# A hybrid decoder step: the gate matrix of the dense expert tiles built by accumulating indirect DMAs of single elements into a cleared DRAM tensor instead of by one-hot products

## The chip, the cores and the metric

The kernel runs on one core of one Trainium2 chip. The core has five engines with an instruction queue each: TensorE (PE, matrix products), VectorE (DVE), ScalarE (ACT), GpSimd (POOL) and SyncE (SP, which here only issues DMAs). Each engine works through its own queue in order, and engines wait for each other by semaphores. DMAs move data between DRAM and the on-chip memory; plain ones are issued from SP, those whose addresses come from a table of indices ("indirect") from POOL. The metric is the time of one execution in microseconds (us).

## What is computed

One layer of a decoder trunk for 1024 prompt tokens (8 tiles of 128) and 32 sample tokens (a ninth tile): a mixing block (windowed attention and a gated recurrence), cross-attention, and a feed-forward layer of 16384 one-neuron experts, from which each token takes 16 for each of 8 heads. The change is in this last layer, `peer_ffn`:

```
q  = (x @ w_pq)                                   # per token: 8 heads
s1, s2 = q_left @ k1, q_right @ k2                # 128 + 128 scores per head
v1, i1 = top_k(s1, 16); v2, i2 = top_k(s2, 16)
sc, ci = top_k(v1[:, None] + v2[None, :], 16)     # 16 of the 256 sums
e = i1[ci // 16] * 128 + i2[ci % 16]              # expert numbers, 0 .. 16383
g = softmax(sc)
y = sum over heads and k of  g * gelu(x . peer_u[e]) * peer_v[e]
```

## The kernel before

The tokens go through the first two blocks in three parts, `PARTS = ((0, 1, 2), (3, 4, 8), (5, 6, 7))`. A part has `middle` (attention and recurrence, four rounds) and `tail` (output product, cross-attention, expert scores, and at its end `select_tile` for each tile, which yields the chosen expert numbers and weights). The generators of the parts are interleaved by `run`, and a list scheduler then puts the instructions of the whole program into an order for each engine; on the chip each engine keeps that order.

The expert layer is done in two ways. Tiles 5, 6, 7 and 8 are gathered: `gather_tile` fetches for every one of a token's choices a row of `peer_u` and then of `peer_v` (128 rows of 4 KB in one indirect DMA, issued by POOL, L1177), and DVE takes the dot product (L1184) or adds the scaled row (L1195). That is 32 + 32 such DMAs for tile 8 and 128 + 128 for each of 7, 6 and 5: 832. Tiles 0 to 4 (`DENSE`, 640 tokens) are done densely: `dense` runs over 128 groups of 128 experts; for each it forms `a = u . x` for all 640 tokens (L202 to L204), gelu (ACT, L1082), multiplies by a gate (DVE, L1084: the softmax weight where the token has chosen the expert, otherwise zero) and multiplies with `v` (L1092 to L1094). While PE does this, POOL and DVE do the gathered tiles.

So `dense` needs a gate matrix of 128 x 128 experts by 640 tokens in DRAM (`gtall`, 42 MB). It is built by `gates(di)`, which takes for each dense tile the two key numbers and the weight of every choice (stored by `select_tile` as `selD`, after three PE transposes), and for each token multiplies two one-hot matrices: DVE builds the first for four tokens at once (L1013) and the second, scaled by the weight, for each token (L1018; for some of the tokens of tiles 2 to 4 ACT does that with two instructions, L1021 and L1022), PE multiplies them (L1024), ACT copies the result out of PSUM (L1027), and SP stores it in pieces of 16 tokens (L1030). `run` interleaves tiles 0 to 2 with part 2's `middle` and tiles 3 and 4 with part 2's `tail`. In `dense` the gates come back in pieces of eight groups of experts (`gate_piece`, L1058).

POOL's other work is 25 small `pow` instructions in `rstd_of` (L211), one in each normalization, which later work on DVE and PE waits for.

## Time and profile before

| | before |
|---|---|
| time, median of 3 runs | 3695.17 us (3675.76 to 3701.54) |
| span of the profiled execution | 3704.7 us |
| PE busy | 3390.1 us (92%) |
| DVE busy | 2623.8 us (71%) |
| ACT busy | 1401.8 us (38%) |
| POOL busy | 1102.0 us (30%) |
| bytes moved by DMA | 1007.87 MB |

The profile cuts the span into 40 slices of 92.6 us and gives for each the busy tenths of each engine, the share of full clock granted to PE, and the busy share of the DMA engines. "Stretches" below are the same sums for windows of one's own choice. The timeline lists instructions in order of time, with the idle time of the engine ahead of each and what ended it. The chain is the sequence of work that ended last, followed back from the end.

### The profile page before, as it was taken

What the parts mean: (1) busy time and instruction counts of PE and PEld (TensorE: products, weight loads), DVE (VectorE), ACT (ScalarE), POOL (GpSimd) and SP (SyncE); (2) the same over time, 40 slices, a digit from 0 to 9 for tenths busy, and PEclk for the clock granted to TensorE, in tenths of its full rate; (3) what the DMA queues carried; (4) which work ended last, traced back from release to release, by engine and by line L of the source; (5) the groups of instructions that cost most, each with busy time, mean ns of one, the idle gap of its engine ahead of it and who ended that gap; (6) DMA issues with size and microseconds to landing.
All of it is one profiled execution on the core that took longest, in us unless ns stands there. A gap on an engine that the chain in (4) does not pass through costs nothing.

```text
span 3704.7 us, 53428 instructions
## 1 busy us (share of the span) xinstructions
PE 3390.1 (92%) x19338; PEld 2927.2 (79%) x19338; DVE 2623.8 (71%) x6014; ACT 1401.8 (38%) x2673; POOL 1102.0 (30%) x871
## 2 busy tenths in 40 slices
PE   5999999999999889886889999999999999999991
PEld 4876776677886779776779988998889998899980
DVE  4443333244885777789878868987788987888996
ACT  4544434343444555886332222222222222222220
POOL 0000000000000000011246535654555555555664
PEclk9999999999999889998999999999999999999995
DMA  7667776665656475489679969998898998999997
GB/s 239 227 226 248 235 256 225 204 208 193 204 190 209 151 266 210 175 317 322 226 259 346 346 229 330 346 334 307 309 325 317 347 344 297 330 339 324 340 329 254
DMA packets 408519, 1007.87 MB, mean 272 GB/s; under 512 B 43968, under 2 KB 168896, under 8 KB 406848
## 3 DMA queue, kind: packets, MB, share of 16 engines
q1 hardware_dynamic: 288448, 568.20, 45.1%
q0 software_dynamic: 119808, 436.26, 32.7%
q8 instruction: 152, 2.49, 0.3%
q14 instruction: 111, 0.91, 0.1%
HBM read 866.01 MB, written 138.31 MB: 271 GB/s over the span
## 4 chain that ended last, share of the span: by engine, by line
PE 27%; DMA 10%; issue 7%; DVE 7%; POOL 4%; ACT 1%; SPq 0%; POOLq 0%; DVEq 0%; ACTq 0%
DMA row<-in_peer_v,ix 5%; PE a L204 4%; PE a L202 4%; PE a L203 4%; POOL row L1177 4%; PE y L1094 3%; PE y L1093 2%; PE y L1092 2%; DMA row<-in_peer_u,ix 2%; PE yr L1092 2%; PE yr L1093 2%; PE yr L1094 2%; DMA u<-in_uT 2%; DVE row L1184 2%; DVE ha L1195 1%
## 5 line engine op out<-in xcount | busy, mean ns | idle before, releaser
L1177 POOL DMA_INDIRECT row<-in_peer_u,ix x416 | 526.2, 1265 | 669.2 <-DVE dots L1184 412.5
L1177 POOL DMA_INDIRECT row<-in_peer_v,ix x416 | 546.4, 1314 | 451.4 <-DVE ha L1195 298.7
L202 PE MATMUL a<-xh,u 128*128 128x320 f32 x2048 | 635.8, 310 | 38.2 <-ACT u L170 28.3
L204 PE MATMUL a<-xh,u 128*128 128x320 f32 x2048 | 635.8, 310 | 2.9 <-DVE u L171 2.9
L203 PE MATMUL a<-xl,u 128*128 128x320 f32 x2048 | 635.5, 310 | 0.0
L1195 DVE SCALAR_TENSOR_TENSOR ha<-row,dots,ha 128x1024 f32<-128x1024 f32 x416 | 533.4, 1282 | 77.0 <-DMA row<-in_peer_v,ix 66.4
L1184 DVE CUSTOM_DVE_ANT_0 row<-row,ha 128x1024 f32<-128x1024 f32 x416 | 501.5, 1222 | 119.7 <-DMA row<-in_peer_u,ix 99.6
L211 POOL TENSOR_TENSOR rs_r<-rs_m,mhalf 128x3 f32<-128x3 f32 (+2 forms) x25 | 21.2, 854 | 1381.7 <-DVE rs_m L209 1083.0
L202 PEld LDWEIGHTS a<-xh,u 128*128 128x128 f32 x2048 | 387.6, 189 | 52.0 <-ACT u L170 28.6
L203 PEld LDWEIGHTS a<-xl,u 128*128 128x128 f32 x2048 | 387.3, 189 | 10.2
L204 PEld LDWEIGHTS a<-xh,u 128*128 128x128 f32 x2048 | 387.3, 189 | 3.6 <-DVE u L171 3.3
L202 PE MATMUL z<-zhi,wz 128*128 128x384 f32 (+2 forms) x928 | 329.1, 355 | 25.8 <-ACT zhi L170 10.2
L203 PE MATMUL z<-zlo,wz 128*128 128x384 f32 (+2 forms) x928 | 316.4, 341 | 2.8 <-DVE zlo L171 2.1
L204 PE MATMUL z<-zhi,wz 128*128 128x384 f32 (+2 forms) x928 | 313.2, 338 | 0.0
L1092 PE MATMUL y<-v,w 128*128 128x512 f32 x768 | 300.9, 393 | 12.4 <-ACT w L170 12.4
L170 ACT CAST w<-w 128x320 fp32r<-128x320 f32 x256 | 117.8, 460 | 503.9 <-DVE w L1084 476.9
L1093 PE MATMUL y<-v,w 128*128 128x512 f32 x768 | 301.3, 394 | 0.0
L170 ACT CAST u<-u 128x1024 fp32r<-128x1024 f32 x128 | 134.8, 1053 | 364.0 <-PE a L203 276.7
L1094 PE MATMUL y<-v,w 128*128 128x512 f32 x768 | 253.7, 392 | 6.5 <-DVE w L171 6.5
L1082 ACT ACTIVATE w<-a 128x320 f32<-128x320 f32 x256 | 110.8, 433 | 361.5 <-PE a L204 337.9
L202 PEld LDWEIGHTS z<-zhi,wz 128*128 128x128 f32 x928 | 180.3, 194 | 65.9 <-issue 19.6
L1092 PE MATMUL yr<-v,w 128*128 128x512 f32 x512 | 204.1, 399 | 19.9 <-DVE ys L1121 15.6
(466 smaller groups left out, 6966.0 us busy)
## 6 DMA issues: line engine op xcount, KB each, us to landing
u<-in_uT SPq DMA_DIRECT2D x128, 512.0 KB
v<-in_peer_v SPq DMA_DIRECT2D x128, 512.0 KB
wz<-wd_w_in SPq DMA_DIRECT2D x112, 512.0 KB
gt<-gtall SPq DMA_DIRECT2D x124, 320.0 KB
wd_w_in<-wz SPq DMA_DIRECT2D x56, 512.0 KB
gtall<-sg SPq DMA_DIRECT2D x34, 512.0 KB
wd_w_pq<-wt SPq DMA_DIRECT2D x32, 512.0 KB
wt<-wd_w_pq SPq DMA_DIRECT2D x32, 512.0 KB
```

The lines of the kernel that those rows point to most:

```text
L170: S.copy(hi, src)
L202: PE.matmul(out, lhsT=whi, rhs=xhi[:, c, sl], start=c == 0, stop=False)
L203: PE.matmul(out, lhsT=whi, rhs=xlo[:, c, sl], start=False, stop=False)
L204: ins = PE.matmul(out, lhsT=wlo, rhs=xhi[:, c, sl], start=False, stop=c == kc - 1)
L211: G.tensor_tensor(r, m, mhalf[:, :n], op=ALU.pow)
L1082: S.activation(ga[:, lo:hi], pa, AF.Gelu)
L1092: PE.matmul(o, lhsT=wh[:, sl], rhs=vh[:, ds], start=start and q == 0, stop=False)
L1093: PE.matmul(o, lhsT=wh[:, sl], rhs=vl[:, ds], start=False, stop=False)
L1094: PE.matmul(o, lhsT=wl[:, sl], rhs=vh[:, ds], start=False, stop=stop and q == len(ws) - 1)
L1177: G.indirect_dma_start(out=row, out_offset=None, in_=tab, in_offset=bass.IndirectOffsetOnAxis(ap=col(ix, j), axis=0))
L1184: V.tensor_tensor_reduce(row, row, hn, 1.0, 0.0, op0=ALU.mult, op1=ALU.add, accum_out=col(dots, j))
L1195: V.scalar_tensor_tensor(acc, row, col(dots, j), acc, op0=ALU.mult, op1=ALU.add)
```

## The change

The gate matrix is now one flat DRAM tensor `gates` of 128 * 128 * 640 elements, ordered by second key, first key, token. Three things make it:

- `clear_gates`, behind `memory_kv` in the first part, stores zeros: 80 DMAs of 512 KB from SP.
- `select_tile` computes for the dense tiles a flat element number, (key2 * 128 + key1) * 640 + token, and stores it and the weight (`ixd`, `gd`, which before were for the gathered tiles only). The transposes, the copies of `selD` and `selD` itself are gone.
- `scatter` loads both and issues 128 indirect DMAs for each dense tile, from POOL, each of which adds one element per token (128 elements) to `gates`. The instructions of a tile that belong to different heads can name the same element and must follow each other; those of one head, and of different tiles, are declared not to conflict. The tables `ix` and `gw` have three buffers, which the gathered tiles also use.

In `dense` the gates of a group of experts are now one DMA of 128 rows of 640 elements, and each waits for the last scatters of all five tiles (`added`). `gates`, `LATE`, `iota`, `selD` and `gtall` are gone. `run` now interleaves the clearing with part 0's middle, `scatter` of tiles 0 to 2 behind part 0's tail with part 1's middle, that of tiles 3 and 4 behind part 1's tail with part 2's middle. The rest of the arithmetic is as before.

```diff
+        eu = T(pk, [128, 128], U32, "sc")[:R, :n]
         if t in DENSE:
-            p = bank(SELB)
-            for i in range(3):
-                PE.transpose(out=p[:, i * 128 : (i + 1) * 128], in_=fnd[:, i], identity=ident)
-            st = T(pk, [128, 4, 128], F32, "c2", 2)
-            ...
-            SP.dma_start(selD[DENSE.index(t)], st)
-            return
-        eu = T(pk, [128, 128], U32, "sc")[:R, :n]
-        V.scalar_tensor_tensor(eu, fnd[:, 0], 128.0, fnd[:, 1], op0=ALU.mult, op1=ALU.add)
+            V.scalar_tensor_tensor(fnd[:, 0], fnd[:, 1], 128.0, fnd[:, 0], op0=ALU.mult, op1=ALU.add)
+            V.tensor_scalar(eu, fnd[:, 0], float(NM), col(TOK, DENSE.index(t)), op0=ALU.mult, op1=ALU.add)
+        else:
+            V.scalar_tensor_tensor(eu, fnd[:, 0], 128.0, fnd[:, 1], op0=ALU.mult, op1=ALU.add)
         SP.dma_start(ixd[t][:R, :n], eu)
         SP.dma_start(gd[t][:R, :n], fnd[:, 2])

-    def gates(di):
-        ...
+    def clear_gates():
+        z = T(pk, [128, 8, 128], F32, "tw", 2)
+        V.memset(z, 0.0)
+        rows = gates.rearrange("(n p x) o -> n p (x o)", p=128, x=1024)
+        for n in range(128 * NM // 1024):
+            SP.dma_start(rows[n], z.rearrange("p a b -> p (a b)"))
+            if n % 10 == 9:
                 yield
+
+    def scatter(dis):
+        ins_ = {}
+        for di in dis:
+            ix = T(gat, [128, 128], U32, "ix", 3)
+            gw = T(gat, [128, 128], F32, "gw", 3)
+            SP.dma_start(ix, ixd[DENSE[di]])
+            SP.dma_start(gw, gd[DENSE[di]])
+            ins_[di] = (ix, gw, [])
+        for h in range(8):
+            for di in dis:
+                ix, gw, last = ins_[di]
+                made = []
+                for j in range(16 * h, 16 * h + 16):
+                    ins = G.indirect_dma_start(out=gates, out_offset=bass.IndirectOffsetOnAxis(ap=col(ix, j), axis=0),
+                                               in_=col(gw, j), in_offset=None, compute_op=ALU.add)
+                    for d in range(len(DENSE)):
+                        for k in range(8):
+                            if d != di or k == h:
+                                tc.declare_no_dep(ins.ins, group=f"gates{d}_{k}", reason="no two of these write one element")
+                    for w_ in last:
+                        sync(ins, w_)
+                    made.append(ins)
+                for ins in made:
+                    tc.add_to_no_dep_group(f"gates{di}_{h}", ins.ins)
+                last[:] = made
+            yield
+        for di in dis:
+            added.extend(ins_[di][2])

         def hidden(i, out):
-            ...
+            gt = T(dn, [128, M], F32, "gt", GTB)
+            ins = SP.dma_start(gt, gview[i])
+            for w_ in added:
+                sync(ins, w_)
...
-                V.tensor_tensor(gv, gv, gts[kg, h][:, :, ki], op=ALU.mult)
+                V.tensor_tensor(ga[:, lo:hi], ga[:, lo:hi], gt[:, lo:hi], op=ALU.mult)

-    run(W0, p[0].middle(lambda: ahead(p[1])), memory_kv())
+    run(W0, p[0].middle(lambda: ahead(p[1])), seq_of(memory_kv, clear_gates))
     p[1].first_h()
-    run(W1, p[1].middle(lambda: ahead(p[2])), seq_of(lambda: p[0].tail("T")), seq_of(sample_mix))
+    run(W1, p[1].middle(lambda: ahead(p[2])), seq_of(lambda: p[0].tail("T"), lambda: scatter(range(NG))), seq_of(sample_mix))
     p[2].first_h()
-    run(W2, p[2].middle(), seq_of(lambda: p[1].tail("T")), seq_of(*[lambda i=i: gates(i) for i in range(NG)]))
-    run(W3, p[2].tail("Z"), seq_of(*[lambda i=i: gates(i) for i in range(NG, len(DENSE))]))
+    run(W2, p[2].middle(), seq_of(lambda: p[1].tail("T"), lambda: scatter(range(NG, len(DENSE)))))
+    run((1,), p[2].tail("Z"))
```

How the order on the engines moves is shown at three places.

**POOL, where the gate of tile 0 starts.** Before, POOL has nothing but `pow` instructions (`rs_r`) here, and then the row gathers of tile 8 (`row<-in_peer_u`):

```order
L211 TENSOR_TENSOR rs_r_8159<-rs_m_8157,mhalf_100 128x3
L211 TENSOR_TENSOR rs_r_9296<-rs_m_9294,mhalf_100 128x3
L211 TENSOR_TENSOR rs_r_9424<-rs_m_9422,mhalf_100 128x3
L211 TENSOR_TENSOR rs_r_10016<-rs_m_10014,mhalf_100 128x3
L211 TENSOR_TENSOR rs_r_11019<-rs_m_11017,mhalf_100 128x3
L211 TENSOR_TENSOR rs_r_11866<-rs_m_11864,mhalf_100 128x3
L211 TENSOR_TENSOR rs_r_13384<-rs_m_13382,mhalf_100 128x3
L211 TENSOR_TENSOR rs_r_13991<-rs_m_13989,mhalf_100 128x3
L1177 DMA row_30090<-in_peer_u,ix_30080 128x1024
```

Now, behind the same `pow` instructions (`rs_r_8621` and `rs_r_9516` stand where 8159 and 9296 stood), the scatters begin (`ix_7742` is tile 0's table, `ix_7746` tile 1's). The semaphores in brackets are those that the row waits for; DMASW0 to DMASW7 are raised in turn when DMAs of POOL have landed, so that the row that waits for DMASW1 waits for the scatter of the row ahead of it:

```order
L203 TENSOR_TENSOR rs_r_9516<-rs_m_9514,mhalf_98 128x3 [waits DVE_49,PE_49]
L1001 DMA gates_158<-gw_7743,ix_7742 10485760x1 [waits DMAHW4_49,DMAHW5_49,DMAHW3_49,DMAHW6_49,DMAHW2_49,DMAHW7_49,DMAHW1_49,DMAHW0_49]
L1001 DMA gates_158<-gw_7743,ix_7742 10485760x1 [waits DMASW0_49]
L1001 DMA gates_158<-gw_7743,ix_7742 10485760x1 [waits DMASW1_49]
L1001 DMA gates_158<-gw_7743,ix_7742 10485760x1 [waits DMASW2_49]
L1001 DMA gates_158<-gw_7743,ix_7742 10485760x1 [waits DMASW3_49]
L1001 DMA gates_158<-gw_7743,ix_7742 10485760x1 [waits DMASW4_49]
```

Every scatter of a tile waits until the scatter ahead of it of the same tile has landed (also within a head); scatters of different tiles alternate. Seven more `pow` instructions stand between the scatters, behind 23, 32, 77, 134, 134, 236 and 305 of them; the last is the last one of part 2's tail. Of these 305 scatters 113 are tile 0's, 102 tile 1's and 90 tile 2's. Tile 3's first scatter stands behind tile 0's last, and tile 4's behind tile 1's.

**POOL and DVE, where `dense` starts.** Now the gathers of tile 8 (64) and of tile 7 (133, `ix_28563`) stand between the scatters of tiles 3 and 4 (`ix_12328`, `ix_12332`):

```order
L1001 DMA gates_158<-gw_12329,ix_12328 10485760x1
L1001 DMA gates_158<-gw_12333,ix_12332 10485760x1
L1142 DMA row_28669<-in_peer_u,ix_28563 128x1024
L1142 DMA row_28672<-in_peer_u,ix_28563 128x1024
L1142 DMA row_28582<-in_peer_u,ix_28563 128x1024
L1142 DMA row_28585<-in_peer_u,ix_28563 128x1024
L1001 DMA gates_158<-gw_12329,ix_12328 10485760x1
L1001 DMA gates_158<-gw_12333,ix_12332 10485760x1
```

From the first scatter to the last there are 844 rows on POOL: 640 scatters, 197 gathers and 7 `pow`. Behind the last scatter comes the gate load, and so the first multiplication by a gate, on DVE. Before, it stood here (`w<-w,gt`; `ha<-row` is a gathered row of tile 8's second half, the 37 ahead of it are all that DVE had taken):

```order
L171 TENSOR_TENSOR v_16183<-v_16180,v_16182 128x1024
L1195 SCALAR_TENSOR_TENSOR ha_30186<-row_30203,dots_30089,ha_30186 128x1024
L1084 TENSOR_TENSOR w_16186<-w_16186,gt_16167 128x320
L1195 SCALAR_TENSOR_TENSOR ha_30186<-row_30206,dots_30089,ha_30186 128x1024
L171 TENSOR_TENSOR w_16188<-w_16186,w_16187 128x320
```

Now it stands here, behind 195 gathered rows (all of tile 8's, and all 128 dot products and three additions of tile 7):

```order
L1157 TENSOR_TENSOR dots_28569<-dots_28569,gw_28564 128x128
L1160 SCALAR_TENSOR_TENSOR ha_28954<-row_28958,dots_28569,ha_28954 128x1024
L1160 SCALAR_TENSOR_TENSOR ha_28954<-row_28961,dots_28569,ha_28954 128x1024
L1160 SCALAR_TENSOR_TENSOR ha_28954<-row_28964,dots_28569,ha_28954 128x1024
L1049 TENSOR_TENSOR w_14360<-w_14360,gt_14346 128x320 x2
L1160 SCALAR_TENSOR_TENSOR ha_28954<-row_28967,dots_28569,ha_28954 128x1024
```

**SP, where `gates` is cleared.** Before, the queue has weight loads of part 0 here (`raw`), stores of their split halves (`wd_w_in`), and `t<-yd`, the first load of part 0's tail:

```order
L190 DMA raw_1480<-in_w_in 128x512
L194 DMA wd_w_in_0_368_1477<-wz_1472 128x1024
L190 DMA raw_1515<-in_w_in 128x512
L493 DMA yd_72_170<-gs_503 128x384
L194 DMA wd_w_in_1_371_1484<-wz_1479 128x1024
```

Now the 80 stores of zeros stand between the loads of `w_mv` and that same `t<-yd`, the last 32 of them without a break:

```order
L978 DMA gates_158<-tw_1422 128x1024 x14
L186 DMA wd_w_in_0_355_1440<-wz_1435 128x1024
L182 DMA raw_1478<-in_w_in 128x512
L978 DMA gates_158<-tw_1422 128x1024 x9
L186 DMA wd_w_in_1_358_1447<-wz_1442 128x1024
L182 DMA raw_1485<-in_w_in 128x512
L978 DMA gates_158<-tw_1422 128x1024 x32
L533 DMA t_3399<-yd_66_163 128x384
```

## Rows read from the trace of the kernel before

**Rows 1.** The page: span; POOL's busy tenths and the DMA rate in 40 slices.
```profile
span 3704.7 us, 53428 instructions
...
POOL 0000000000000000011246535654555555555664
...
GB/s 239 227 226 248 235 256 225 204 208 193 204 190 209 151 266 210 175 317 322 226 259 346 346 229 330 346 334 307 309 325 317 347 344 297 330 339 324 340 329 254
```
**Rows 2.** Stretches of the span: busy us of each engine, PE's granted clock, DMA.
```profile
core 0: us, PE busy (x) PEld busy (x) DVE busy (x) ACT busy (x) POOL busy (x), PEclk, DMA share, GB/s
...
1053.00:1300.00 247.00, 222.60 (x1451) 183.54 (x1450) 174.58 (x593) 127.54 (x238) 4.37 (x5) 0.96 0.53 186
1300.00:1470.00 170.00, 153.45 (x1011) 142.69 (x1010) 120.68 (x530) 94.52 (x240) 0.00 (x0) 0.93 0.72 247
1470.00:1600.00 130.00, 109.34 (x690) 100.51 (x688) 99.48 (x303) 109.66 (x261) 11.45 (x10) 0.95 0.58 212
...
1735.00:2100.00 365.00, 320.09 (x1752) 288.98 (x1752) 311.48 (x688) 106.02 (x154) 164.81 (x122) 0.93 0.84 293
...
3300.00:3600.00 300.00, 299.39 (x1680) 272.53 (x1679) 265.13 (x339) 79.19 (x130) 183.16 (x139) 1.00 0.93 333
```
**Rows 3.** Stretches, the one-hot products alone (L1024): their sum over 1053 to 1735 us.
```profile
sum 682.00, PE 193.09 PEld 173.08; mean PE 48.27 PEld 43.27
```
**Rows 4.** Groups by line: busy us, mean ns, idle before and its releasers.
```profile
L1018 DVE TENSOR_SCALAR oh<-iota,x_vs 128x128 f32<-128x128 f32 x448 | 128.7, 343 | 2.8 <-DMA x_vs<-selD 2.8
...
L1013 DVE TENSOR_TENSOR raw<-iota,x_vs 128x512 f32<-128x512 f32 x160 | 110.2, 688 | 84.8 <-PE g L1024 73.9 <-DMA x_vs<-selD 3.7 <-PE x L1024 3.6
...
L1177 POOL DMA_INDIRECT row<-in_peer_v,ix x416 | 546.4, 1314 | 451.4 <-DVE ha L1195 298.7 <-issue 39.7 <-DMA row<-in_peer_v,ix 35.1
```
**Rows 5.** Timeline of SP: start us, us; the stores of tiles 0 and 3.
```profile
1053.27 0.32 SPq L980 DMA_DIRECT2D selD<-c  x1
...
1524.48 0.32 SPq L980 DMA_DIRECT2D selD<-c  x1
```
**Rows 6.** Timeline of POOL: the last normalization of part 2's tail; gathers back to back.
```profile
1570.81 0.90 POOL L211 TENSOR_TENSOR rs_r<-rs_m,mhalf 128x3 f32<-128x3 f32 x1
...
1904.05 0.94 POOL L1177 DMA_INDIRECT row<-in_peer_u,ix  x1 [0.30 <-issue]
1905.30 0.94 POOL L1177 DMA_INDIRECT row<-in_peer_u,ix  x1 [0.30 <-issue]
```
**Rows 7.** The same with little else running: every gather from here is one row.
```profile
3642.87 1.58 POOL L1177 DMA_INDIRECT row<-in_peer_v,ix  x1 [0.19 <-issue]
...
3670.85 1.68 POOL L1177 DMA_INDIRECT row<-in_peer_v,ix  x1 [0.30 <-issue]
```
**Rows 8.** Chain in order of time: start us, us from issue to landing.
```profile
1806.22 6.68 DMA row<-in_peer_v,ix
...
1838.67 3.46 DMA ixd<-sc
...
2220.53 3.98 DMA row<-in_peer_u,ix
```
**Rows 9.** Instructions on `gt` and `yr`: ns min/median/max, first and last start us.
```profile
L1084 DVE TENSOR_TENSOR w<-w,gt x256: 471/485/544, 1776.0 to 3605.2; 128x320 f32<-128x320 f32 x128
...
L1121 DVE TENSOR_TENSOR ys<-ys,yr x130: 665/681/689, 1795.7 to 3624.8; 128x512 f32<-128x512 f32 x130
```
**Rows 10.** Timeline of SP in part 0: two weight loads, and the tail's first load.
```profile
210.67 0.42 SPq L190 DMA_DIRECT2D raw<-in_w_in  x1
222.91 0.32 SPq L194 DMA_DIRECT2D wd_w_in<-wz  x1
...
233.36 0.77 SPq L541 DMA_DIRECT2D t<-yd  x1
```
**Rows 11.** Stretches of part 0, all engines.
```profile
200.00:340.00 140.00, 126.96 (x664) 96.16 (x663) 61.97 (x189) 60.58 (x135) 2.40 (x3) 0.98 0.69 232
340.00:500.00 160.00, 159.91 (x930) 114.85 (x931) 51.90 (x174) 63.40 (x115) 2.37 (x3) 1.00 0.77 247
```

More of the change, by code (lines that the diff above doesn't have):

```diff
@@ L26 @@
 NG = sum(t in PARTS[0] for t in DENSE)
-GT = 16
+NM = 128 * len(DENSE)
 def col(p, n):
@@ L35 @@
 XA = (16, 1)
-GA = (10, 1)
+GTB = 6
 EARLY = 90
@@ L153, in _body @@
     gd = [T(dr, [128, 128], F32, f"gd{t}") for t in range(9)]
-    selD = [T(dr, [128, 4, 128], F32, f"selD{t}") for t in range(len(DENSE))]
     h3x = [T(dr, [128, 8, 128 * len(DENSE)], F32, f"h3x{i}") for i in range(2)]
-    gtall = T(dr, [len(DENSE) * 128 // GT, 128, 128 * GT], F32, "gtall")
+    gates = T(dr, [128 * 128 * NM, 1], F32, "gates")
     accd = T(dr, [128, D], F32, "accd")
-    gtd = [gtall[b].rearrange("p (i t) -> p i t", t=GT) for b in range(len(DENSE) * 128 // GT)]
     mkd = T(dr, [128, 4, 256], F32, "mkd")
@@ L667, in tail @@
                     if smp:
-                        sc4 = T(wk, [128, 2, 128], F32, "sc4")
+                        sc4 = c2([128, 2, 128])
                 q = tq(jc % 2)
@@ L984, in select_tile @@
         SP.dma_start(ixd[t][:R, :n], eu)
         SP.dma_start(gd[t][:R, :n], fnd[:, 2])
-    flips = {}
-    def flip(name, n):
-        flips[name] = flips.get(name, -1) + 1
-        return flips[name] % n
-    def gates(di):
-        st = T(wk, [128, 4, 128], F32, "x_vs")
-        SP.dma_start(st, selD[di])
-        late_ = di >= NG
-        for blk in range(128 // GT):
-            if late_:
-                k = flip("stg", 3)
-                if k < 2:
-                    stg = [T(wk, [128, 128, GT], F32, ("thi", "tlo")[k])]
-                else:
-                    stg = [T(wk, [128, 64, GT], F32, "sg", 2) for i in range(2)]
-            elif flip("stg", 2) or not BIG:
-                stg = [T(wk, [128, 64, GT], F32, "sg", 2) for i in range(2)]
-            else:
-                stg = [T(gat, [128, 64, GT], F32, "row", 2) for i in range(2)]
-            w = 128 // len(stg)
-            for q in range(GT // 4):
-                p = bank(("g", "Ty", "Ts")[flip("gb", LB)] if late_ else "g")
-                t0 = blk * GT + 4 * q
-                hot = [T(wk, [128, 4, 128], F32, "raw" if RAW else "oh", 2 if RAW else 3), T(wk, [128, 4, 128], F32, "oh", 3)]
-                V.tensor_tensor(hot[0], iota.rearrange("p (o k) -> p o k", o=1).to_broadcast([128, 4, 128]),
-                                st[:, 0, t0 : t0 + 4].rearrange("p (t o) -> p t o", o=1)
-                                .to_broadcast([128, 4, 128]), op=ALU.is_equal)
-                for i in range(4):
-                    if i >= LATE[di]:
-                        V.tensor_scalar(hot[1][:, i], iota, col(st[:, 1], t0 + i), col(st[:, 2], t0 + i),
-                                        op0=ALU.is_equal, op1=ALU.mult)
-                    else:
-                        S.activation(hot[1][:, i], iota, AF.Abs, bias=col(st[:, 1], t0 + i), scale=-1.0)
-                        S.activation(hot[1][:, i], hot[1][:, i], AF.Relu, bias=col(st[:, 2], t0 + i),
-                                     scale=col(st[:, 3], t0 + i))
-                    PE.matmul(p[:, i * 128 : (i + 1) * 128], lhsT=hot[0][:, i], rhs=hot[1][:, i],
-                              start=True, stop=True)
-                for i, sg in enumerate(stg):
-                    ANY.tensor_copy(sg[:, :, 4 * q : 4 * q + 4].rearrange("p i t -> p t i"),
-                                    p.rearrange("p (t i) -> p t i", i=128)[:, :, i * w : (i + 1) * w])
-            for i, sg in enumerate(stg):
-                SP.dma_start(gtd[di * (128 // GT) + blk][:, i * w : (i + 1) * w], sg)
-            if blk % 2:
-                yield
@@ new lines, in clear_gates, with sync @@
+    def clear_gates():
[5 more added lines that the diff above has]
+            if n % 10 == 9:
+                yield
+    added = []
+    def sync(ins, to):
+        tc.add_manual_dep(ins.ins, to.ins.name,
+                          mybir.DependencyInfo(mybir.DependencyClass.Sync, mybir.DependencyReason.DATA), reason="gates")
@@ L1077, in hidden @@
                 lo, hi = h * (M // 2), (h + 1) * (M // 2)
-                kg, ki = divmod(i + 4 * h, 8)
-                ki -= 4 * h if kg == 0 else 0
                 pa = T(dps, [128, 512], F32, "a", 6 - 2 * KEEP + 1 if KEEP > 2 else 2)[:, : M // 2]
```

39 lines of the change are left out of this document (6 added, 33 removed).

## The prediction

> **What bounds the kernel now.** I read the page first, for when POOL works and how fast DMA can go, then stretches of the span, then the groups by line, and for single events the timelines, the chain and the view by tile.
>
> POOL does next to nothing in the first 17 of 40 slices and has room later; the fastest slices move 346 GB/s [rows 1]. From 1053 to 1600 us PE is busy 222.60 + 153.45 + 109.34 = 485 of 547 us, with DVE at 72% [rows 2]: a mixed stage in which no engine is full. The one-hot products take 193 us of PE from 1053 to 1735 us [rows 3]; DVE's two lines for them take 128.7 + 110.2 = 239 us [rows 4]. From then on `dense` runs. Its first multiplication by a gate is at 1776.0, and the last product is added at 3624.8 us [rows 9]; deep in it PE is busy 299 of 300 us [rows 2]. The end, at 3704.7 us, is late gathers of tile 5 and the sample's finish. So two questions decide: when can `dense` begin, and how long does it then run.
>
> **What the change takes away.** All of the one-hot work: 193 us of PE, 239 us of DVE, and ACT's share, all between 1053 and 1735 us. If nothing else ended later, `dense` could begin 100 to 190 us earlier: PE's 193 us is the most, and the stretch from 1735 to 2100 us with 45 us of idle PE [rows 2] shows that the start of `dense` has other limits.
>
> **What it adds, 1: clearing.** 80 stores of 512 KB, 42 MB, at the best 346 GB/s [rows 1] are 121 us of transfer. On SP they stand between the `w_mv` loads and `t<-yd`; before, this piece of the queue took from about 211 to 233 us [rows 10]. The weight loads of part 0 are queued behind them. DMA was busy 0.69 there, and from 340 us PE is busy 159.91 of 160 us [rows 11], so a delay isn't made good. Bounds: 0 (all in the gaps) and 121 us; I take 70, since 23 us of the old queue time and some 30 us of work that needs no new weights lie beside it. So the first scatter, which stands behind tile 0's `select_tile` at 1053.27 us [rows 5], can start at about 1053 + 70, say 1125.
>
> **What it adds, 2: 640 scatters on POOL.** Each issues 128 addresses, as a gather does, but 4 bytes for each instead of 4 KB. The trace has no such DMA. Its price has two parts. *Issue*: a gather holds POOL 0.94 us with 0.30 to the next at best [rows 6], 1.31 + 0.30 in the mean [rows 4]. I take 1.24 to 1.37 (a scatter moves almost nothing, but is issued by the same engine in the same form). *Landing*: the shortest landing of a gather that the chain shows is 3.98 us after its issue, another 6.68; a small store to DRAM took 3.46 [rows 8]. For a scatter I take 3.5, nearest to the small store; bounds 2.5 (two issues, if landing costs less) and 6.7.
>
> The order says what these cost. Every scatter of a tile waits for the one before it of that tile to have landed. So time goes in rounds, one scatter of each tile that is being scattered, and a round lasts as long as its issues or as a landing, whichever is longer:
>
> - A, up to the last `pow`: 12 rounds of tile 0 alone and 12 of two tiles, 3.5 us each; 89 of three tiles, 3 x 1.37 = 4.1 us each. 84 + 365 = 449 us. Part 2's normalizations (the last was at 1570.81 us [rows 6]) stand on POOL between these scatters, so PE's work of parts 1 and 2, though some 190 us less, cannot run ahead of them: the relief is lost here.
> - B, up to tile 8's first gather: 38 rounds of about three, 4.1 us: 156.
> - C, with one gather of tile 8 in each: 64 rounds of three issues, 3.9 us: 250.
> - D1, 27 rounds with four gathers of tile 7: six issues at 1.24 are 7.4 us; four gathers at the pace of the late ones (16 intervals from 3642.87 to 3670.85 us, 1.75 each [rows 7]) and the two scatters behind them are 9.5. I take 8.5: 230.
> - D2, 24 rounds with one gather, 3.5 us: 84.
>
> The last scatter lands at 1125 + 449 + 156 + 250 + 230 + 84 = 2294 us. What waits for it: the first gate load on SP, with every gate load and half of the `u` loads queued behind it; then DVE's first multiplication, ACT's split, and all of PE, which has nothing else left. PE and the transfers stand still from the end of part 2's tail on.
>
> A rule of the Trainium skill (DMA: Bandwidth & Descriptors, section Anatomy of one DMA, SWDGE path) puts such a DMA at about 2.0 us fixed plus its bytes at 436 GB/s, the fixed part being mostly the receipt of the write. By that estimate the rounds that I price by a landing would cost 2.5 us (their two issues) or less instead of 3.5, and the sum would fall by about 50 us; the gather of 3.98 us [rows 8] would by the same rule have taken 3.2, so here the trace is slower than the rule, and I keep the row.
>
> **`dense` itself.** From first multiplication to last addition it took 3624.8 - 1776.0 = 1849 us [rows 9]. It now has 637 gathers beside it instead of 795, all done when 4/5 of it are over, the three selections of tiles 5 to 7 are out of its start (45 us of idle PE), and the gate load has rows of 2560 bytes. Against that the gathers are denser while they last. I take 1829; PE nearly full deep in it says that not much more is to be had, so bounds 1800 and 1860. Behind it stand the final norms of the dense tiles, 26 us (20 to 40); the 80 us of late gathers at the end are gone.
>
> **The sum.** 2294 + 4 (gate load) + 1829 + 26 = 4153 us of span, against 3704.7. The median of the runs is 9.5 below the profiled span, so about 4145.
>
> Low end of the parts: no delay by the clearing (1053), 24 rounds at 2.5, triple rounds at 3.72, D1 at 7.44, D2 at 2.48: last scatter at 2084, span about 3,910. High end: clearing 121, every round a landing of 6.7, D1 at 9.5: A 757, B 255, C 429, D1 257, D2 161, last scatter at 3033, span about 4,900.
>
> **Rivals.**
> *Slow element adds.* An add must read the old value before it writes, and all three tiles' adds go through one queue; a round is then a landing of 6.7 us or more and the span about 4,900. For it: nothing in the trace adds; the gathers of the chain often take 6 to 7 us [rows 8]. Against it: those carry 512 KB. Chance 0.13, from about 4,550 up.
> *The scatters hide.* The other side: if issue and landing are cheap enough, the last scatter is in time. It decides at one point: the span is 3704.7 again when the last scatter lands at 3705 - 1859 = 1846 us. From 1125 us that leaves 721 us for 844 rows on POOL, 0.85 us each, gaps included; from 1053, 0.94. The back-to-back gathers take 1.24 [rows 6]. And even with free scatters the 133 gathers of tile 7 stand ahead of the last ones, behind that tile's selection, at 1.75 us [rows 7] some 230 us: so it ends at no change, about 3,690, not at a gain. For it: a scatter moves 512 bytes. Chance 0.05, of which 0.02 for faster.
> *Half hidden.* POOL issues a scatter in less time than a gather (say 0.6 + 0.3), so that rounds cost a landing of 2.5 to 3 us: A 300, B 103, C 195, D1 200, D2 60; last scatter at 1983, span about 3,840. Chance 0.10.
> Forecast as summed: 0.72.
>
> **How the numbers follow.** The likeliest is 4145. Below 3,930 lie the two cases in which the scatters hide or half hide (0.12 of their 0.15); above 4,550 lies most of the slow adds (0.10). So 3,930 to 4,550 holds a little under 8 in 10. A change of about 1% is what a measurement of this kernel can tell from none: slower by over 1% has 0.95, within 1% 0.03, faster 0.02.
>
> **What would show it.** In the trace after: no one-hot lines; POOL busy without a break from about 1.1 ms, with PE's slices at zero between the end of part 2's tail and about 2.3 ms; the first multiplication by a gate there, released by the gate load, which was released by a scatter. Scatter to scatter in three-tile rounds about 1.37 us, POOL waiting for its own DMAs in the rounds of one and two tiles. In part 0, SP's piece with the zeros lasting about 120 us, and tile 0's selection at about 1125. `dense` at about 1830 us and no gathers at its end. I am wrong if `dense` starts before 1.9 ms, or if a scatter's landing is over 6 us.

## The result, and the profile after

| | before | after |
|---|---|---|
| median of the runs, us | 3698.4 (3675.8 to 3704.3) | 4546.9 (4543.3 to 4557.2) |
| span of the profiled execution, us | 3704.7 | 4542.1 |
| PE busy, us | see the table of before | 3237.2 |
| POOL busy, us | see the table of before | 2112.6 |
| first multiplication by a gate, us | 1776.0 | 2741.9 |
| last addition of `dense` begins, us | 3624.8 | 4526.6 |

The change makes the kernel slower: 1.230 times the time before (95% interval 1.225 to 1.234). Forecast were 4145 us, with 3930 to 4550 for the range. The sign and what bounds held; the size is 400 us short, and the time lies 3 us inside the upper end of the range.

The page of the changed kernel, first its span, then busy tenths of PE, of POOL and PE's granted clock in 40 slices, then the group of the scatters:

```profile
span 4542.1 us, 50244 instructions
...
PE   6569999999774943600000008999999999999998
...
POOL 0000000000587887888888886656555565553000
...
PEclk9789999999886976855555558999999999999999
...
L1001 POOL DMA_INDIRECT gates<-gw,ix x640 | 1032.5, 1613 | 301.7 <-issue 172.8
```

(The dots stand for lines left out.) PE has zeros in slices 18 to 24, where POOL stands at 8; before, POOL's first busy slice was the 18th [rows 1]. One stretch of the changed kernel, from the last work of part 2 to the last scatter (busy us and instructions of PE, PEld, DVE, ACT, POOL; PE's granted clock; DMA share; GB/s), shows what this hole is:

```profile
2010.00:2730.00 720.00, 0.00 (x0) 0.00 (x0) 264.75 (x456) 9.42 (x8) 593.62 (x410) 0.50 0.55 143
```

For 720 us PE executes nothing, and its granted clock reads 0.50, the lower of its two levels. POOL's 594 us are 82% of the stretch and the rest is its 0.3 us between two issues. The end of the hole, in the chain of waits (start us, us, what):

```profile
2731.58 0.99 POOL row L1142
2732.58 2.63 issue
2735.44 3.60 DMA gates<-gw,ix
2739.18 2.71 DMA gt<-gates
2741.91 0.50 DVE w L1049
```

It is the chain that was forecast: the last scatter is issued, lands after 3.60 us, releases the first gate load, and that releases the first multiplication. Before, that multiplication came at 1776.0 us [rows 9]; so the start of `dense` went back by 966 us, and 837 us of it are left at the end.

What a scatter costs, by its line (ns min/median/max of one; what its engine waited for; landing), and two of them from POOL's timeline:

```profile
L1001 POOL DMA_INDIRECT gates<-gw,ix x640: 1532/1542/2599, 1145.0 to 2735.4; - x160
...
  issue: 172.8, 568
  DMA gates<-gw,ix: 88.2, 70
...
DMA to landing us min/median/max: 2.9/3.3/8.9
```

```profile
1300.57 1.54 POOL L1001 DMA_INDIRECT gates<-gw,ix  x1 [0.30 <-issue]
1302.41 1.54 POOL L1001 DMA_INDIRECT gates<-gw,ix  x1 [0.30 <-issue]
```

A gather back to back took 0.94 + 0.30 [rows 6], a scatter takes 1.54 + 0.30 = 1.84. Of the 1590 us between the first scatter and the last, POOL waited only 88 for scatters to land: the price is in the issue, not in the landing.

Last, the instructions on the gates, the additions, and the stores of the selected indices (nine tiles; the first is tile 0's), each with first and last start:

```profile
L1049 DVE TENSOR_TENSOR w<-w,gt x256: 476/484/561, 2741.9 to 4509.5; 128x320 f32<-128x320 f32 x128
```
```profile
L1086 DVE TENSOR_TENSOR ys<-ys,yr x130: 674/680/689, 2753.6 to 4526.6; 128x512 f32<-128x512 f32 x130
```
```profile
L970 SPq DMA_DIRECT2D ixd<-sc x9: 319/320/423, 1138.3 to 2090.4; - x9
```

`dense` is 4526.6 - 2741.9 = 1785 us long, 64 less than before. Tile 0's selection ends at 1138 us, 85 later than before [rows 5].

### The profile page after: what moved, and what is told of

It reads as the page before. It is cut to its first block, busy times and chain, and to the rows that moved or that the text cites. A ratio compares the mean times of both kernels' runs of the same rounds, so it can differ in the third digit from the quotient of the medians.

```text
span 4542.1 us, 50244 instructions
## 1 busy us (share of the span) xinstructions
PE 3237.2 (71%) x18043; PEld 2786.4 (61%) x18043; DVE 2427.6 (53%) x5411; ACT 1113.9 (25%) x2004; POOL 2112.6 (47%) x1511
## 3 DMA queue, kind: packets, MB, share of 16 engines
q0 software_dynamic: 211968, 436.63, 32.4%
## 4 chain that ended last, share of the span: by engine, by line
PE 52%; POOL 22%; DMA 11%; issue 9%; SPq 2%; DVE 2%; ACT 1%; POOLq 0%; DVEq 0%; ACTq 0%
POOL gates L1001 17%; DMA gates<-gw,ix 6%; PE a L195 6%; PE a L196 6%; PE a L194 6%; POOL row L1142 5%; PE y L1058 3%; PE y L1057 3%; PE y L1059 3%; PE yr L1058 2%; PE yr L1057 2%; PE yr L1059 2%; PE z L194 2%; PE z L196 2%; PE z L195 2%
## 5 line engine op out<-in xcount | busy, mean ns | idle before, releaser
L1001 POOL DMA_INDIRECT gates<-gw,ix x640 | 1032.5, 1613 | 301.7 <-issue 172.8
L1057 PE MATMUL y<-v,w 128*128 128x512 f32 x768 | 302.1, 393 | 821.2 <-ACT w L162 821.2
L1057 PEld LDWEIGHTS y<-v,w 128*128 128x128 f32 x768 | 145.0, 189 | 848.0 <-ACT w L162 822.6
L1142 POOL DMA_INDIRECT row<-in_peer_u,ix x416 | 512.8, 1233 | 302.1 <-DVE dots L1149 203.6
L194 PE MATMUL z<-zhi,wz 128*128 128x384 f32 (+2 forms) x928 | 333.6, 360 | 189.4 <-ACT wz L162 84.9
L196 PE MATMUL z<-zhi,wz 128*128 128x384 f32 (+2 forms) x928 | 318.8, 344 | 0.0
L1058 PE MATMUL y<-v,w 128*128 128x512 f32 x768 | 302.4, 394 | 0.0
L1059 PE MATMUL y<-v,w 128*128 128x512 f32 x768 | 264.8, 391 | 2.6 <-DVE w L163 2.6
L163 DVE TENSOR_TENSOR u<-u,u 128x1024 fp32r<-128x1024 f32 x128 | 156.5, 1223 | 171.8 <-ACT u L162 171.5
```

The costliest lines, as they stand in the source:

```text
L163: V.tensor_tensor(lo, src, hi, op=ALU.subtract)
L194: PE.matmul(out, lhsT=whi, rhs=xhi[:, c, sl], start=c == 0, stop=False)
L196: ins = PE.matmul(out, lhsT=wlo, rhs=xhi[:, c, sl], start=False, stop=c == kc - 1)
L1001: ins = G.indirect_dma_start(out=gates, out_offset=bass.IndirectOffsetOnAxis(ap=col(ix, j), axis=0), in_=col(gw, j), in_offset=None, compu ...
L1057: PE.matmul(o, lhsT=wh[:, sl], rhs=vh[:, ds], start=start and q == 0, stop=False)
L1058: PE.matmul(o, lhsT=wh[:, sl], rhs=vl[:, ds], start=False, stop=False)
```

## The experiments

Two theories to begin with. **Issue**: POOL pays 1.84 us for each scatter, whatever the DMA does behind it. **Landing**: the waits of a tile's scatters for each other set the pace. Later a third came up, **mutual wait**: POOL's normalizations stand in line with the scatters, PE's part 2 needs the normalizations, and the scatters need what PE computes. Each kernel of this part was executed once. Times are spans of the profiled execution; the kernel before had spans of 3707 to 3713 us beside these runs, and all its executions took 3676 to 3715 us, so that a difference in span of less than some 40 us shows nothing by itself.

### What the add costs: plain

```
-   in_=col(gw, j), in_offset=None, compute_op=ALU.add)
+   in_=col(gw, j), in_offset=None)
```

> The changed kernel with one word taken out: the scatters write instead of adding, so an element that several heads hit keeps one head's weight. Rows, waits and the order on POOL stay the same. In the changed kernel a scatter holds POOL 1.54 us, with 0.30 us to the next; a gather at its best 0.94. Theory 'the add is dear to issue': without it a scatter holds POOL 0.94 us as a gather does; with its 0.30 us that is 0.60 us less for each of 640, at most 384 us, so the last scatter is at about 2350 us instead of 2735 and the span about 4160. Theory 'the form is dear' (4-byte elements, or the scattering direction): 1.54 us again, last scatter within 20 us of 2735, span within 20 us of 4542.

The span is 4448.1 us. The scatters' line, and what POOL waited for from 1597 to 2000 us (us, times, longest):

```profile
L1001 POOL DMA_INDIRECT gates<-gw,ix x640: 952/958/2372, 1149.5 to 2645.2; - x160
```
```profile
POOL rs_r L203 <- DVE rs_m L201: 135.4, 2, 84.2
```

Without the add the scatter holds POOL 0.96 us, a gather's price: the add alone costs 0.58 us of issue. But of the 384 us that this should give back only 94 came. In the changed kernel POOL never waited for a normalization's input after the first scatter; here it does so for 135 us in this stretch and for 221 us in all, and the last normalization comes at 1827.7 us, in the changed kernel at 1768.7. Waits for landings are 19 us longer than there (107.2 against 88.2), and the load of a tile's weights is waited for 26.5 us.

The normalizations' inputs are late for the most part because PE, DVE and ACT stand still together while POOL goes on. The longest such stretch (columns as above), and what ACT waited for at its end:

```profile
1547.00:1604.00 57.00, 0.00 (x0) 0.00 (x0) 0.00 (x0) 0.00 (x0) 38.94 (x41) 0.50 0.04 10
```
```profile
ACT q L662 <- remote: 68.1, 2, 63.0
```

The trace calls a wait "remote" when it shows nobody who raised the semaphore. Between the first scatter and the last normalization there are eight such stretches of 8 to 58 us, 160 us in sum. PE's order is the same as in the changed kernel, whose trace has no wait of this kind, nor has that of any other run. What these stretches are, and whether a second execution would have them, stays open; so `plain` shows the price of the add, but not what the kernel would take without it.

### No landing waits within a head: free

```
-for ins in made:
-    tc.add_to_no_dep_group(f"gates{di}_{h}", ins.ins)
```

and the line that enters a scatter in its group stands inside the loop, right behind the scatter:

```
+    tc.add_to_no_dep_group(f"gates{di}_{h}", ins.ins)
     made.append(ins)
```

> The changed kernel, but the 16 scatters of one head and tile no longer wait for each other (no two of them write one element); a head still waits for the head before it. The order on POOL changes with it: the scatters stand nearly in one piece and 2 instead of 197 gathers are ahead of the last one. Theory 'issue': POOL's price per scatter decides, 640 x 1.84 = 1178 us, so the last scatter is at 1145 + 1178 + some 10 = about 2330 us, dense begins there, span about 2330 + 1807 = 4140, and a scatter still holds POOL 1.54 us. Theory 'landing': the waits were what made a scatter dear; then a scatter costs clearly less than 1.84 us here (1.24 as a gather: 794 us, last scatter about 1945, and dense then begins where part 2's tail lets it, span 3750 to 3900).

The span is 4509.4 us and the last scatter is at 2529 instead of 2330; a scatter still holds POOL 1.54 us. Both theories missed. The stretch from 1500 to 1800 us (columns as above), and POOL's longest wait behind it:

```profile
1500.00:1800.00 300.00, 0.00 (x0) 0.00 (x0) 0.00 (x0) 0.00 (x0) 250.27 (x164) 0.50 0.24 0
```
```profile
POOL rs_r L203 <- DVE rs_m L201: 149.3, 1, 149.3
```

For 300 us no engine but POOL does anything. In this order two normalizations stand behind the first 96 scatters and the next four behind 288 more; PE has finished what needed the two and stands until the four are reached (421 us in one wait for a normalization), and then POOL stands 149 us for the input of the next. That is the mutual wait. The DMA share of 0.24 at 0 GB/s belongs to the scatters too: 512 bytes each, which round to nothing.

### Half of the scatters: half

```
-for h in range(8):
+for h in range(4):
```

> The changed kernel with only heads 0 to 3 scattered, 320 scatters instead of 640 (the weights of heads 4 to 7 are left out of the gates); the order on POOL is the scheduler's for that: 391 rows from the first to the last scatter, 64 gathers of tile 8 and 7 normalizations among them, none of tile 7. Theory 'a price for each row': the changed kernel's rows took 1590 us for 844, 1.88 each; 391 rows then take 737 us, the last scatter is at about 1145 + 737 = 1880, and the span about 1880 + 1807 = 3690. Rival 'something else than POOL holds dense back once it is late' (parts 1 and 2 of PE's work, the gathers): the span stays more than 100 us above that.

The span is 3862.6 us, not 3690, so the rival came true: the last of 391 rows is at 2049, 2.30 us a row instead of 1.88. Between 1145 and 2052 us POOL waited for

```profile
POOL gates L1001 <- DMA gates<-gw,ix: 180.0, 101, 5.0
```

That is 180 us for half the scatters, against 88 for all; that fewer scatters stand abreast, so that their landing shows, would fit, but was not tested. PE still waits 95 us for normalizations. A price for each row is a floor, not the time.

### Normalizations off POOL: actpow, freeact

```
-G.tensor_tensor(r, m, mhalf[:, :n], op=ALU.pow)
+S.activation(r, m, AF.Ln)
+S.activation(r, r, AF.Exp, scale=-0.5)
```

On the changed kernel alone (actpow), and on top of `free` (freeact).

> The changed kernel with one thing changed: the 25 normalizations are computed on ScalarE instead of on POOL, so that no pow stands among the scatters (838 rows on POOL instead of 844, 198 gathers among them; the waits between scatters stay). Theory 'POOL's prices set the last scatter': POOL was busy or issuing nearly all the time from 1145 to 2735 us, it never waited for a normalization's input there, so the last scatter stays between 2690 and 2750 and the span between 4490 and 4560. Rival 'the normalizations behind scatters cost the time' (PE and POOL waiting for each other): the last scatter comes over 100 us earlier, span under 4440.

> As the run 'free' (scatters of one head and tile don't wait for each other), and the 25 normalizations of the parts, which POOL computes with pow, are computed by ScalarE from a logarithm and an exponential, so that none stands between scatters on POOL. In 'free' PE stood still from 1500 to 1800 us behind one pow that had 280 scatters ahead of it, and POOL then waited 149 us for the next pow's input. Theory 'mutual wait': without pows on POOL the 640 scatters run through, 640 x 1.84 = 1178 us, last one at about 1145 + 1180 = 2325, PE's part 2 is done before 1900, span about 2325 + 1807 = 4130. Rival 'the scatters themselves slow down' (queue or memory full): last scatter after 2450 and span over 4250, with no PE work left to blame.

`actpow`: span 4575.1 us, last scatter at 2765.7, each some 15 us above what the first theory allowed and far from the rival's. Taking the normalizations off POOL brings nothing as long as POOL's rows are dear and stand in this order; in the changed kernel itself the mutual wait is not what costs the time.

`freeact`: the scatters run through, 640 in 1217 us, 1.90 each, the last at 2376.3 (2325 had been expected). The span is 4382.8, not 4130. Scatters, gates and the gathers of this kernel:

```profile
L1002 POOL DMA_INDIRECT gates<-gw,ix x640: 1552/1563/2673, 1159.7 to 2376.3; - x160
```
```profile
L1049 DVE TENSOR_TENSOR w<-w,gt x256: 476/485/559, 2384.2 to 4220.3; 128x320 f32<-128x320 f32 x128
```

`dense` begins 358 us earlier than in the changed kernel, but the span ends only 159 us earlier. All 832 gathers now stand behind the scatters: the first is at 2378, the last at 4348 us. They run beside `dense` to its end, `dense` lasts 1859 us from first multiplication to last addition, and what is left of the gathers ends the kernel. In their 1970 us POOL waits 759 us for DVE, which works on the gathered rows (419.2 for its dot products, 339.7 for its sums), so it is POOL and DVE by turns that set their pace. POOL's line is one: what is taken from the scatters' wait comes back as late gathers. PE also stood still from 1700 to 1900 us, without a normalization to blame; the waits of SP (1150 to 2376 us) and of PE (1500 to 2100 us):

```profile
SPq L994 <- DMA gates<-gw,ix: 256.2, 7, 239.6
```
```profile
PE z L194 <- DMA wz<-wd_w_pq: 241.1, 1, 241.1
```

The tables of indices have three buffers. The load of the fourth tile's table waits on SP until a tile's scatters are done, and weight loads are queued behind it. It cost nothing here, since the scatters end later than PE's part 2.

### Both together, without the add: plainact

`freeact` with the edit of `plain`.

> As 'freeact' (no landing waits within a head, normalizations on ScalarE), and the scatters write instead of adding (an element that several heads hit keeps one head's weight). In 'freeact' 640 scatters ran in one piece at 1.90 us each, and behind them POOL needed 2007 us to the end for its 832 gathers. In 'plain' a scatter that writes held POOL 0.96 us and came every 1.26. Theory 'POOL is one queue of prices': scatters 640 x 1.27 to 1.32 = 813 to 845 us, last one at about 1160 + 830 = 1990, dense begins there, the gathers end 2007 us later: span 3980 to 4010. Rival 'PE's part 2 becomes the bound' (its weight loads stood on SP behind the loads of the scatter tables for 241 us in 'freeact'): dense begins after 2080, span over 4060.

The span is 3991.4 us, as POOL's prices said, and `dense` does not wait for PE's part 2. Scatters, then the gathers of the second table:

```profile
L1002 POOL DMA_INDIRECT gates<-gw,ix x640: 954/958/1980, 1150.8 to 1983.8; - x160
```
```profile
L1142 POOL DMA_INDIRECT row<-in_peer_v,ix x416: 934/1018/2079, 2103.6 to 3958.4; - x139
```

833 us for the scatters instead of 1217, and 391 us less of span. With the normalizations and the landing waits out of the way the add's 0.58 us appears in full, 0.60 x 640 = 384; in `plain` a quarter of it did. This trace has none of the unexplained waits of `plain`.

### What the rest of the change is worth: noscat, bare

```
-for h in range(8):
+for h in range(0):
```

This is `noscat`; `bare` has two edits more:

```
-seq_of(memory_kv, clear_gates)
+seq_of(memory_kv)
...
-ins = SP.dma_start(gt, gview[i])
+ins = SP.dma_start(gt, A["uT"][i].rearrange("p a b -> p (a b)")[:, :M])
```

> The changed kernel without the 640 scatters (the gates stay zero, so the dense tiles' expert sums are left out of the output; all else, clearing included, is there). It shows what the change would have been worth with scatters for nothing. Theory 'relief': the one-hot work of 193 us of PE stood on the path, so dense begins at 1776 + 85 (clearing) - 193 = about 1670 us and the dense tiles end near 3470; the end is then the late gathers, which start 85 us later than before: span 3700 to 3790 less what dense gives back. Theory 'no relief': other limits set the start of dense: it begins at about 1860, the dense tiles end near 3665, span about 3750.

> As the run without scatters, but without the clearing too; the gate loads, of the same shape and size, read a table of inputs instead (the dense tiles' expert sums are left out of the output in effect). The difference to the run without scatters is the clearing alone. Theory 'clearing delays all that follows': tile 0's selection comes 85 us earlier (1053 instead of 1138 us) and the span is about 85 us shorter. Rival 'the delay is made good later': the selection comes 85 us earlier, but the span is less than 30 us shorter.

Spans 3640.0 and 3551.0 us. The stores of indices of the two (first start is tile 0's), `noscat` first:

```profile
L970 SPq DMA_DIRECT2D ixd<-sc x9: 319/320/424, 1139.1 to 1860.0; - x9
```
```profile
L970 SPq DMA_DIRECT2D ixd<-sc x9: 319/326/424, 1050.7 to 1786.1; - x9
```

and the multiplications by a gate, `noscat` first:

```profile
L1049 DVE TENSOR_TENSOR w<-w,gt x256: 466/484/562, 1736.3 to 3527.6; 128x320 f32<-128x320 f32 x128
```
```profile
L1049 DVE TENSOR_TENSOR w<-w,gt x256: 470/485/561, 1644.5 to 3437.2; 128x320 f32<-128x320 f32 x128
```

`dense` of `noscat` begins between the two times that were expected, and its span is below the figures of both theories. `bare` shows the theory's 85 us. This is the account of the change, in spans: 3704.7 before (3712.9 in the execution beside these two); 153.7 less when the one-hot work is gone and nothing takes its place (`dense` begins 131.5 us earlier); 89.0 more for clearing; 902.1 more for the scatters; 4542.1 after. The clearing's delay of 88 us at tile 0's selection passes whole to the end. With scatters for nothing the kernel would have been some 65 us faster than before, not far above what single executions can tell: the forecast's rival gave 3690 for that case, with tile 7's gathers ahead of the last scatter, and without scatters the scheduler doesn't put them there.

### Where the clearing's 89 us come from: actclear, pace1

In `actclear`:

```
-SP.dma_start(rows[n], z.rearrange("p a b -> p (a b)"))
+S.dma_start(rows[n], z.rearrange("p a b -> p (a b)"))
```

In `pace1`, where `cur[0]` is the latest split of a weight chunk:

```
-SP.dma_start(rows[n], z.rearrange("p a b -> p (a b)"))
-if n % 10 == 9:
+sync(SP.dma_start(rows[n], z.rearrange("p a b -> p (a b)")), cur[0])
+if n % 1 == 0:
```

> The changed kernel with the 80 clearing stores issued from ScalarE's queue instead of SP's. Theory 'SP's order': the weight loads of part 0 no longer stand behind the stores, so tile 0's selection comes at about 1060 us instead of 1138 and the span is about 80 us shorter, 4460. Rival 'bytes': 42 MB take their transfer time from part 0's weight loads by whichever queue they go: selection at 1120 to 1145, span within 20 us of 4542.

> The changed kernel with each of the 80 clearing stores tied to a weight split of part 0 and so spread along SP's queue (half of them behind place 260 of the queue instead of all before place 200). Without any clearing tile 0's selection came 89 us earlier than with it. Theory 'queue': weight loads waited behind stores that came in one piece; spread out they hide, the selection comes at 1050 to 1080 instead of 1138, the last scatter some 70 us earlier, span about 4470. Rival 'bytes': 42 MB cost their transfer time wherever they stand: selection at 1120 to 1140, span within 20 us of 4542.

Spans 4587.2 and 4553.4 us. The clearing stores of `actclear` and of `pace1`:

```profile
L978 ACTq DMA_DIRECT2D gates<-tw x80: 326/1244/1951, 142.4 to 251.0; - x80
```
```profile
L980 SPq DMA_DIRECT2D gates<-tw x80: 319/1229/1795, 148.4 to 428.1; - x80
```

In `actclear` they leave SP, but tile 0's selection is no earlier, 1153.9 us, and the span is 45 us longer. In `pace1` the selection comes at 1123.0, 15 us earlier. Both theories of a queue missed; the figures of the rival hold in `pace1` and are passed by 9 and 25 us in `actclear`. But neither edit takes the stores out of the way. The changed kernel and `pace1`, in the stretch where PE does least (columns as above):

```profile
200.00:250.00 50.00, 9.12 (x24) 7.28 (x24) 3.22 (x7) 3.19 (x5) 0.00 (x0) 0.50 1.02 407
```
```profile
380.00:420.00 40.00, 0.00 (x0) 0.00 (x0) 0.00 (x0) 0.00 (x0) 0.00 (x0) 0.50 1.02 407
```

and the waits there, of the changed kernel (150 to 262 us), of `actclear` (the same) and of `pace1` (340 to 440 us):

```profile
ACT wz L162 <- DMA raw<-in_w_in: 49.8, 4, 31.5
ACT thi L162 <- DMA t<-yd: 36.8, 1, 36.8
```
```profile
ACT wz L162 <- DMA gates<-tw: 62.0, 3, 33.1
```
```profile
PE z L196 <- DMA wz<-wd_w_in: 61.2, 1, 61.2
```

In the changed kernel ACT waits 87 us for loads of part 0 that SP issues between and behind the stores. In `actclear` the stores fill ACT's own queue, 1.2 us each, and its conversions of weights stand behind them. In `pace1` 73 of the 80 stores still stand nearly in one piece, from 334.9 to 429.4 us, and PE waits for a weight load behind them. So in all three the price is paid in a queue behind stores, and the transfer sets how long they last: 42 MB at the 407 GB/s of these stretches are 103 us. That the bytes cost as much wherever they stand is not shown. In `hyb2s` (below) 32 of these stores, tied as in `pace1` (25 of them still stand in one piece), leave tile 0's selection at 1057.4 us, 4 later than before, where two fifths of 85 would be 34. Stores that are spread out in fact were not tried with the full 42 MB.

### Mixtures: hyb2, hyb2s

Tiles 0 and 1 by scatters, 2 to 4 by one-hot products. The gates are read from two tensors, and the multiplication of `dense` has two pieces, first the tokens of tiles 0 and 1, then the others as before the change:

```
+V.tensor_tensor(ga[:, lo:sc_], ga[:, lo:sc_], gs[:, lo:sc_], op=ALU.mult)
 V.tensor_tensor(gv, gv, gts[kg, h][:, :, ki], op=ALU.mult)
```

> A mixture: tiles 0 and 1 by scatters (256 of them, free within a head), tiles 2 to 4 by one-hot products as before the change; the cleared tensor is 2/5 as large and its 32 stores are spread; normalizations on ScalarE as in 'freeact'. 256 x 1.84 = 471 us from about 1100 end at about 1570, before dense can begin. Theory 'relief': without all one-hot work and clearing dense began 132 us earlier (1644 against 1776); two fifths of that are 53 us, less at most 35 for clearing: dense begins at 1723 to 1760, span 3640 to 3690. Rival 'POOL and DMA get in the way': the one-hot stage keeps its length, and the span is 3705 or more.

> A second mixture: tiles 0 and 1 by 256 scatters, tiles 2 to 4 by one-hot products, 32 clearing stores spread out, normalizations left on POOL, scatters of a tile wait for each other as in the changed kernel (then the scheduler spreads the normalizations among the scatters: the six of them at rows 26 to 214 of 287). In the first mixture the normalizations on ScalarE needed 20 table loads of 1.28 us, and PE was busy only 57% from 1450 to 1650 us. Theory 'relief': dense begins at 1720 to 1760, span 3640 to 3690. Rival 'any scatters on POOL stretch the stage that holds PE's part 2': dense begins after 1780, span 3700 or more.

Spans 3737.4 and 3823.3 us. The first multiplications by a scattered gate, `hyb2` first:

```profile
L1148 DVE TENSOR_TENSOR w<-w,gs x128: 400/419/469, 1835.8 to 3626.7; 128x256 f32<-128x256 f32 x128
```
```profile
L1148 DVE TENSOR_TENSOR w<-w,gs x128: 400/420/496, 1930.3 to 3724.6; 128x256 f32<-128x256 f32 x128
```

Both rivals came true: `dense` begins later than before the change, by 60 and 154 us, though the scatters were done at 1570 and 1717. From 1450 to 1650 us PE was busy 113 us in `hyb2`, and 165 before. Among its waits are 53 us for DVE, in `hyb2s` 54 us for ACT and 37 for a normalization behind scatters. Which of these waits decides was not settled. No run that computes all gates was faster than the kernel before.

## Why the prediction was right, and where it was short

**The range: right by luck.** The median, 4546.9 us, lies 3 us under the upper end of 4550, and one of the four runs, 4557.2, above it. That end stood where the rival of slow adds begins, not where a sum of the forecast's own terms ends, and what carried the time there is for the most part the price of the add: by its 0.47 to 0.60 us over the forecast's issue, 300 to 384 us for 640 scatters, of the 389 that are missing.

**What bounds, and the sign: right.** The forecast rested on POOL being idle early and on what waits for the last scatter. The trace shows both: the chain from scatter to gate load to first multiplication, PE at zero from 2.0 to 2.7 ms, and no gathers at the end of `dense` (the last is at 4158 us). Neither of the two signs of being wrong came: `dense` starts at 2742 us, not before 1900, and a landing takes 3.3 us in the median, not over 6. The break-even of the rival in which the scatters hide, 0.85 us a row on POOL, was never near: rows took 1.88.

**Clearing: right.** 70 us were taken, within 0 and 121; it was 85, and 89 by the pair of runs. The reason given (weight loads queued behind the stores on SP) is what the trace shows: ACT waits 87 us for such loads. Moving the stores to ACT's queue gained nothing, since ACT's work then stands behind them. The upper bound rested on 346 GB/s; the stores moved at 407.

**Relief: right.** 100 to 190 us were given for a `dense` that nothing else delays; it is 131.5.

**Landing: right.** 3.5 us were taken, between 2.5 and 6.7; the median is 3.3, the shortest 2.9, the longest 8.9. The Trainium skill (DMA: Bandwidth & Descriptors, section Anatomy of one DMA, SWDGE path) has 2.0 us for such a small DMA; no scatter here came that low, and the measurement decides.

**Issue: the term that failed.** It was priced at 1.24 to 1.37 us with its gap, on the ground that a scatter is issued by the same engine in the same form as a gather. It cost 1.84, and `plain` and `plainact` show that the ground held for a scatter that writes (1.26) and not for one that adds. The rival with slow adds looked for their price in the landing, so it named the right cause and the wrong place. The rounds, measured by the same marks (first scatter, last pow, first gather, start of the first and end of the last group of four gathers, start of the last scatter), us:

| | forecast | after | plain |
|---|---|---|---|
| first scatter | 1125 | 1145 | 1150 |
| A, to the last normalization | 449 | 624 | 678 |
| B, to tile 8's first gather | 156 | 233 | 205 |
| C, one gather in a round | 250 | 351 | 276 |
| D1, four gathers in a round | 230 | 266 | 240 |
| D2, one gather in a round | 84 | 116 | 97 |
| last scatter | 2294 | 2735 | 2645 |

In C, D1 and D2 the forecast's working, with a price that it had right for `plain`, comes within 26 us in each; the add explains the rest there. In the changed kernel the add's price also explains A: 305 scatters at 1.84 are 561 of the 624 us where the forecast has 449, waits for landings are most of the rest, and taking the normalizations away (`actpow`) doesn't bring the last scatter forward. In `plain` B is 49 us over the forecast, 26 of them the wait for a tile's weights, and A doesn't get shorter at all: POOL waits 221 us for normalizations' inputs, and these are late for the most part by the stretches, 160 us in sum, whose cause is open. A was made from POOL's rows alone. `free` shows that such a sum can miss a wait of PE and POOL for each other; how much of one `plain` would have without those stretches isn't known. Taken out whole, they would leave about 4290 us (an estimate: 4448 less 160), and not 4145, as the time with the issue as it was forecast.

**`dense`: too long.** 1829 us were taken, 1800 the least; it is 1785. In `bare`, with gate loads of the same form and nearly all gathers still beside it, it is 1813 (from 1644.5 to 3457.4 us). So some 36 us come with the new form of the gate loads and the end of the one-hot work, which were not told apart, and the other 28 would fit the gathers that are done before `dense` begins (200 of them, in `bare` 42), which no run tests alone. Behind it 15 us stood where 26 were forecast.

The sum, then: 445 us too little up to the landing of the last scatter (2739 us), 1 too much for the gate load, 44 and 11 too much behind it: 389, the difference of 4542 to 4153.

## What to carry to other kernels

Price an operation by a row of the same operation, and where there is none, take its whole form into the bound: a DMA that adds is not a DMA that writes, and the difference can sit on the issuing engine. When work moves to an idle engine, look for the small instructions that already stand in that engine's line: they are late from then on, whatever they are. And look at what the idle engine has to do later: what is put ahead of it in the same line moves it back.

## What the runs showed of the hardware

The add costs the issue: medians of 1.54 to 1.56 us in every kernel where it stood (the changed one, `free`, `half`, `freeact`, `actpow` and both mixtures), with DVE busy or idle, against 0.96 in the two where the scatter writes. The Trainium skill (DMA: Bandwidth & Descriptors, section SWDGE vs HWDGE vs iDMA) says that for DMAs from POOL a program on that engine writes the descriptors; a price that depends on the kind of DMA and not on its bytes (0.94 us for a gather of 512 KB, 0.96 for a scatter of 512 bytes that writes) agrees with that, and no run shows what the program does differently. The records of POOL's queue differ as well (packets, MB, share; the changed kernel, `plain`, `noscat`):

```profile
q0 software_dynamic: 211968, 436.63, 32.4%
```
```profile
q0 software_dynamic: 140288, 436.63, 28.5%
```
```profile
q0 software_dynamic: 119808, 436.26, 33.6%
```

Less the gathers' 119808, a scatter that adds leaves (211968 - 119808) / 640 = 144 packets and one that writes 32. But a gather leaves 119808 / 832 = 144 too and is issued in 0.94 us, so the number of packets alone is not what the issue costs.
